# Strided attention: weight columns that interleave two head parities, and stores of every second row in 16 KiB reads

## The chip, the core and the metric

The kernel runs on one core of one Trainium2 chip. The metric is the device time of one execution in microseconds, median of three runs. The core has five engines that run side by side and wait for each other through semaphores: TensorE (PE, matrix products into PSUM; its weight loads are PEld in the profile), VectorE (DVE), ScalarE (ACT), GpSimd (POOL) and SyncE (SP), which here only issues DMA transfers. Sixteen DMA engines move data between DRAM and SBUF, the on-chip memory of 128 partitions.

## The reference

Eight batches of twelve heads, 1024 queries of 64 numbers each. Every query attends to the same 16 keys of its head, at positions 0, 64, ..., 960. All is float32 in DRAM.

```python
batch, heads, seq, dim = (8, 12, 1024, 64)          # stride 64
attend_positions = np.arange(0, seq, stride)        # 16 keys
scores = einsum('bhqd,bhkd->bhqk', q, k) / sqrt(dim)
weights = exp(scores - max); weights /= sum(weights) + 1e-10
result[:, :, i, :] = einsum('bhqk,bhkd->bhqd', weights, v)
```

Q is 25.2 MB and the result is 25.2 MB. Of K and V only 16 rows a head are read, 0.39 MB each.

## The kernel before

The 96 heads are worked on in 24 groups of four heads (HG = 4). A group's Q is 1 MiB: 128 partitions of 8 KiB in tile `qn`. The result of a group is as large: `out_sb`, also 8 KiB in each of 128 partitions.

**Layout.** The four heads of a group are numbered 0 to 3; the parity `a` of a head is its number modulo two. A head has 64 blocks of 16 queries. In `qn` a partition holds 32 queries of one head, so two blocks (x); a block falls into two halves (e) of eight queries (t). In `out_sb`, partition 64a + q holds block q of the two heads of parity a, 4 KiB for each. So in `store` (L250) one partition is read as 8 KiB and written as two pieces of 4 KiB, 512 KiB apart in DRAM, and the 128 partitions form one regular row of steps.

**A group's chain.** `cast` (L199, GpSimd) turns Q into bf16. `transpose` (L203, VectorE) transposes blocks of 32 by 32 pairs of bf16 numbers. `scores` (L205) makes four matmuls of 512 columns (L210) that add up in one PSUM bank: 64 partitions for each parity, and columns ordered by query t, then x, then q, the partition from which the query came. ScalarE takes the exponential of each half (L221) and writes it into the weight buffer `w`: eight matrices of 128 by 128, in which the rows of parity a fill only the columns of parity a, 64a and up; the rest was set to zero once. `values` (L191, GpSimd) lays the values side by side for the four combinations of head and half that a parity has, each in the rows of its own keys, with four more columns of ones that give the sums. `outputs` (L228) multiplies in three blocks, for 3, 2 and 3 of the eight t (L235): column p of a weight matrix becomes partition p of the product. For each block VectorE takes the reciprocal of the sums (L243); in the blocks of three it also multiplies and writes to `out_sb` (L245), and in the block of two ScalarE copies (L247) and GpSimd multiplies (L248). PSUM has two buffers for these products, so the third block's matmuls wait for the first block's L245.

**Order.** The schedule is written by hand. SyncE issues K, load 0, V and loads 1 to 7 at once (QBUFS = 8). Loads 0 and 1 read 128 rows of 8 KiB, later ones 32 rows of 32 KiB (L93). In the loop over g, `ahead(g)` puts in transpose(g + 2), scores(g + 1), values(g + 2) and cast(g + 3), then come the three `outputs`, then `store(g)` and `load(g + 8)`. All transfers leave from one queue, so a load stands behind the store ahead of it. A store waits on SyncE until all three blocks of its group are written. A group's first write to `out_sb` waits for the store of nine groups earlier (OBUFS = 9). In five of the groups from 1 to 7 the keys of later groups are prepared as well (L156 to L169), and in group 4 the second half of the values (L177).

The softmax here doesn't subtract the row's maximum and nothing guards it: scores larger than these inputs give would overflow.

## Time and profile before

| | |
|---|---|
| time, median of three (range) | 129.17 us (128.92 to 129.61) |
| span of the profiled execution | 127.6 us |
| busy: PE, DVE, ACT, POOL | 67.2, 95.5, 57.5, 90.3 us |
| DMA: packets, bytes, mean rate | 7910, 51.19 MB, 401 GB/s |
| issue to landing, median: loads, stores | 11.7, 9.8 us |
| first and last issue of a store | 20.6, 119.9 us |

The profiler's span is shorter than the measured time by some 1.6 us (the profiled execution took 129.27 us). The stretch rows of the page cut the span in 40 slices and give the busy share of each in tenths; PEclk is the clock that TensorE was granted. The rows of groups give, for one line of code, count, busy time, mean duration and the idle time of the engine before it. The timeline gives start and duration of single instructions, and in brackets the engine's idle time before one and what ended it. For a DMA issue the trace also tells how long it took from issue to landing; transfers of one queue land in the order of their issue here. The page's groups that the change touches:

```profile
L235 PE MATMUL o_ps<-v,w 128*128 128x260 bf16 x192 | 40.0, 333 | 36.1 <-DVE out_sb L245 34.5
L221 ACT ACTIVATE w<-sc 64x512 bf16<-64x512 f32 x48 | 35.3, 735 | 30.1 <-PE sc L210 28.3
L210 PE MATMUL sc<-qt,k_t 128*128 128x512 bf16 x96 | 33.3, 479 | 12.8 <-DVE qt L203 11.6
```

### The profile page before, as it was taken

What the parts mean: (1) busy time and instruction counts of PE and PEld (TensorE: products, weight loads), DVE (VectorE), ACT (ScalarE), POOL (GpSimd) and SP (SyncE); (2) the same over time, 40 slices, a digit from 0 to 9 for tenths busy, and PEclk for the clock granted to TensorE, in tenths of its full rate; (3) what the DMA queues carried; (4) which work ended last, traced back from release to release, by engine and by line L of the source; (5) the groups of instructions that cost most, each with busy time, mean ns of one, the idle gap of its engine ahead of it and who ended that gap; (6) DMA issues with size and microseconds to landing.
All of it is one profiled execution on the core that took longest, in us unless ns stands there. A gap on an engine that the chain in (4) does not pass through costs nothing.

```text
span 127.6 us, 1150 instructions
## 1 busy us (share of the span) xinstructions
PE 67.2 (53%) x292; PEld 30.1 (24%) x292; DVE 95.5 (75%) x167; ACT 57.5 (45%) x96; POOL 90.3 (71%) x89
## 2 busy tenths in 40 slices
PE   0005267766456796436757565379734877365100
PEld 0002032233222343212423232124221433132000
DVE  6947557788898678898879888897889878977300
ACT  4110614576771458776445653543554626462100
POOL 8962489877898286898888888898689887433300
PEclk9999999999955558999756999955999657998555
DMA  2999989898998998999989989999999999999980
GB/s 68 378 319 468 462 360 483 349 483 362 460 465 352 480 455 339 506 385 393 501 344 447 460 375 450 426 403 457 442 380 455 439 393 421 424 426 424 429 360 26
DMA packets 7910, 51.19 MB, mean 401 GB/s; under 512 B 3872, under 2 KB 3872, under 8 KB 3872
## 3 DMA queue, kind: packets, MB, share of 16 engines
q1 hardware_dynamic: 7904, 51.12, 96.7%
q8 instruction: 2, 0.03, 0.1%
q14 instruction: 4, 0.03, 0.1%
HBM read 25.95 MB, written 25.17 MB: 401 GB/s over the span
## 4 chain that ended last, share of the span: by engine, by line
DVE 48%; DMA 16%; PE 14%; issue 9%; POOL 4%; SPq 1%; ACT 0%; DVEq 0%; POOLq 0%
DVE out_sb L245 30%; PE o_ps L235 11%; DVE qt L203 10%; DMA out_dram<-out_sb 9%; DMA qn<-in_Q_dram 7%; DVE rec L243 7%; PE sc L210 3%; POOL out_sb L248 2%; POOL qb L199 1%; DVE v_rep L184 1%; SPq L35 1%; POOL v L191 1%; ACT out_sb L247 0%; SPq L100 0%; DVE k_r L159 0%
## 5 line engine op out<-in xcount | busy, mean ns | idle before, releaser
L235 PE MATMUL o_ps<-v,w 128*128 128x260 bf16 x192 | 40.0, 333 | 36.1 <-DVE out_sb L245 34.5
L221 ACT ACTIVATE w<-sc 64x512 bf16<-64x512 f32 x48 | 35.3, 735 | 30.1 <-PE sc L210 28.3
L199 POOL CAST qb<-qn 128x2048 bf16<-128x2048 f32 x24 | 45.3, 1889 | 4.2 <-DMA qn<-in_Q_dram 4.2
L245 DVE TENSOR_TENSOR out_sb<-o_ps,rec 128x768 f32<-128x768 f32 x48 | 46.0, 958 | 1.7
L248 POOL TENSOR_TENSOR out_sb<-out_sb,rec 128x512 f32<-128x512 f32 x24 | 25.0, 1042 | 22.2 <-ACT out_sb L247 22.2
L210 PE MATMUL sc<-qt,k_t 128*128 128x512 bf16 x96 | 33.3, 479 | 12.8 <-DVE qt L203 11.6
L235 PEld LDWEIGHTS <-w 128*128 128x128 bf16 x192 | 18.7, 113 | 63.5 <-DVE out_sb L245 48.1
L203 DVE STREAM_TRANSPOSE qt<-qb 128x1024 int32<-128x1024 int32 x24 | 29.6, 1233 | 4.7 <-POOL qb L199 4.7
L243 DVE RECIPROCAL rec<-o_ps 128x12 f32<-128x12 f32 (+1 forms) x72 | 15.3, 212 | 15.9 <-PE o_ps L235 15.8
L247 ACT COPY out_sb<-o_ps 128x512 f32<-128x512 f32 x24 | 14.0, 585 | 24.9 <-DVE rec L243 12.1
L191 POOL TENSOR_TENSOR v<-mask,v_rep 128x256 bf16<-128x256 bf16 x24 | 16.0, 669 | 2.3 <-DVE v_rep L184 2.3
L210 PEld LDWEIGHTS <-k_t 128*128 128x128 bf16 x96 | 10.8, 113 | 23.8 <-issue 10.7
L169 ACT COPY k_t<-k_r 32x128 bf16<-32x128 bf16 x20 | 5.9, 295 | 2.2 <-DVE k_r L159 1.9
L129 POOL MEMSET k_t<- 128x4608 bf16 x1 | 3.9, 3937 | 0.0
L180 PE MATMUL vp<-v_bf,perm_v 128*128 128x384 bf16 x4 | 1.8, 513 | 2.4 <-DVE v_rep L184 2.4
L139 DVE TENSOR_SCALAR s_sel<-col,slot_f 128x4 bf16<-128x4 int16 x1 | 2.5, 2546 | 0.1
L158 ACT CAST k_bf<-k_raw 128x256 bf16<-128x256 f32 x3 | 1.2, 405 | 3.1 <-DMA k_raw<-in_K_dram 3.0
L184 DVE CAST v_rep<-vp 128x384 bf16<-128x384 f32 x4 | 2.1, 543 | 0.6 <-PE vp L180 0.6
L123 DVE MEMSET k_t<- 128x1152 uint32 x1 | 1.0, 1018 | 1.0 <-PEq L311 1.0
L158 ACT ACT_TABLE_LOAD x1 | 1.3, 1283 | 0.7 <-PEq L311 0.7
L127 DVE MEMSET w<- 128x512 uint32 x3 | 1.5, 485 | 0.2
L118 POOL COPY perm_v<-identity 128x32 bf16<-128x32 bf16 x8 | 1.2, 209 | 0.0
(16 smaller groups left out, 5.0 us busy)
## 6 DMA issues: line engine op xcount, KB each, us to landing
qn<-in_Q_dram SPq DMA_DIRECT2D x24, 1024.0 KB, 11.7
out_dram<-out_sb SPq DMA_DIRECT2D x24, 1024.0 KB, 9.8
k_raw<-in_K_dram SPq DMA_DIRECT2D x1, 384.0 KB, 4.3
v_raw<-in_V_dram SPq DMA_DIRECT2D x1, 384.0 KB, 7.3
```

The costliest lines, as they stand in the source:

```text
L129: nc.gpsimd.memset(k_t[:, 8:NG], 0.0)
L169: op(k_t[dst : dst + 32, 8 * m + c : 8 * m + 8 : 2, :, col : col + NK], k_r[src : src + 32, 4 * m : 4 * m + 4].rearrange("p n (a k f) -> p ...
L191: nc.gpsimd.tensor_tensor(out=vb[g][:, 0 : 4 * D].rearrange("p (s d) -> p s d", s=4), in0=mask, in1=v_rep[:, g // 2, g % 2].unsqueeze(1).t ...
L199: nc.gpsimd.tensor_copy(out=qb[g], in_=qn[g])
L203: nc.vector.transpose(qt[g].bitcast(I32), qb[g].bitcast(I32))
L210: nc.tensor.matmul(sc, lhsT=k_t[:, g, f, NK * (1 - e) : NK * (1 - e) + P], rhs=_ap_with(q, [q.ap[0], [D, 8], [16 * D, 2], [2, 32]], extra_ ...
L221: nc.scalar.activation(out=_ap_with(wa, [wa.ap[0], [P, 8], [1, 2], [2, 32]], extra_offset=64 * a), in_=sc[64 * a : 64 * a + 64].rearrange( ...
L235: nc.tensor.matmul(ps[:, i, 0 : 4 * D + 4], lhsT=wt[g][:, i0 + i], rhs=vb[g], start=True, stop=True,)
L243: nc.vector.reciprocal(r, ps[:, 0:n, 4 * D : 4 * D + 4])
L245: nc.vector.tensor_tensor(out=to, in0=o, in1=by, op=ALU.mult)
L247: nc.scalar.copy(to, o)
L248: nc.gpsimd.tensor_tensor(out=to, in0=to, in1=by, op=ALU.mult)
```

## The change

The weight matrices get their columns interleaved: the rows of parity a fill the columns 2q + a. For that the score matmul reads its moving operand in another order (x innermost, in steps of 16 * D elements, that is 2 KiB), so that the score columns come out by t, then by block of 16 queries, and the exponential writes every second column. Partition 2q + a of a group's result now holds block q of parity a.

The result tiles hold two groups: 16 KiB in a partition, four such tiles (OBUFS = 4) in place of nine of 8 KiB. A store takes the partitions of one parity, 64 of them in steps of two, and both groups: 16 KiB read at a time, written as four pieces of 4 KiB. It is 1 MiB as before, and there are still 24. Both stores of a pair are issued after the odd group, each followed by a load. Q gets ten buffers, so that ten loads are issued ahead. The change is for fewer and longer DMA reads.

```diff
-    QBUFS = 8
-    OBUFS = 9
+    QBUFS = 10
+    OBUFS = 4
...
                     rhs=_ap_with(
-                        q, [q.ap[0], [D, 8], [16 * D, 2], [2, 32]],
+                        q, [q.ap[0], [D, 8], [2, 32], [16 * D, 2]],
                         extra_offset=8 * D * e + f,
                     ),
...
             nc.scalar.activation(
-                out=_ap_with(wa, [wa.ap[0], [P, 8], [1, 2], [2, 32]], extra_offset=64 * a),
-                in_=sc[64 * a : 64 * a + 64].rearrange("p (t x q) -> p t x q", t=8, x=2),
+                out=_ap_with(wa, [wa.ap[0], [P, 8], [2, 64]], extra_offset=a),
+                in_=sc[64 * a : 64 * a + 64].rearrange("p (i q) -> p i q", i=8),
                 func=AF.Exp, bias=0.0, scale=scale,
             )
...
         if c == 0:
-            out_sb[g] = out_pool.tile([P, 4, 8, D], FP32, name="out_sb", tag="out_sb")
+            if g % 2 == 0:
+                out_2[g // 2] = out_pool.tile(
+                    [P, 2, 4, 8, D], FP32, name="out_sb", tag="out_sb"
+                )
+            out_sb[g] = out_2[g // 2][:, g % 2]
...
-    def store(g):
-        o = out_sb[g]
+    def store(n, a):
+        o = out_2[n][a : P : 2]
         _copy(
             nc,
-            _ap_with(out, [[16 * D, P], [2 * SD, 2], [1, 16 * D]], g * HG * SD),
-            _ap_with(o, [o.ap[0], [1, 1], [1, 32 * D]]),
+            _ap_with(
+                out, [[16 * D, 64], [2 * SD, 4], [1, 16 * D]],
+                2 * n * HG * SD + a * SD,
+            ),
+            _ap_with(o, [o.ap[0], [1, 1], [1, 64 * D]]),
         )
...
-        store(g)
-        if g + QBUFS < NG:
-            load(g + QBUFS)
+        if g % 2 == 1:
+            for a in range(2):
+                store(g // 2, a)
+                if g - 1 + a + QBUFS < NG:
+                    load(g - 1 + a + QBUFS)
```

## The prediction

> **What bounds the kernel now.** I read the page's DMA rows first:

> ```profile
> DMA  2999989898998998999989989999999999999980
> ...
> DMA packets 7910, 51.19 MB, mean 401 GB/s; under 512 B 3872, under 2 KB 3872, under 8 KB 3872
> ...
> q1 hardware_dynamic: 7904, 51.12, 96.7%
> ```

> The 16 DMA engines are busy from the second slice to the last but one, and the queue's packets fill 96.7% of their time. 7904 less 3872 small ones leaves 4032 large packets. They fit the reads: 24 stores of 128 reads of 8 KiB (3072), loads 0 and 1 of 128 (256) and 22 loads of 32 reads of 32 KiB (704). So a packet is counted per read, and stores are three quarters of the large ones.

> Second, the engines, since a last store can't leave before its data. VectorE over one group, and its last instruction:

> ```profile
> 77.05 0.96 DVE L245 TENSOR_TENSOR out_sb<-o_ps,rec 128x768 f32<-128x768 f32 x1
> 77.92 0.20 DVE L243 RECIPROCAL rec<-o_ps 128x8 f32<-128x8 f32 x1
> 78.61 0.23 DVE L243 RECIPROCAL rec<-o_ps 128x12 f32<-128x12 f32 x1 [0.49 <-PE o_ps L235]
> 78.88 0.96 DVE L245 TENSOR_TENSOR out_sb<-o_ps,rec 128x768 f32<-128x768 f32 x1
> 79.75 1.23 DVE L203 STREAM_TRANSPOSE qt<-qb 128x1024 int32<-128x1024 int32 x1
> 80.91 0.20 DVE L243 RECIPROCAL rec<-o_ps 128x12 f32<-128x12 f32 x1
> 81.14 0.96 DVE L245 TENSOR_TENSOR out_sb<-o_ps,rec 128x768 f32<-128x768 f32 x1
> ...
> 118.82 0.96 DVE L245 TENSOR_TENSOR out_sb<-o_ps,rec 128x768 f32<-128x768 f32 x1
> ```

> A group takes 81.14 - 77.05 = 4.09 us, with one real gap, 0.49 us for the third block's matmuls. No wait for a DMA stands in VectorE's rows after 23 us, so this chain runs by itself to 119.78 us. The chain of waits shows an 11.52 us step "DMA out_dram<-out_sb" at 100.79 us; VectorE is busy all through it, so I don't take it for a stall.

> Third, the end: SyncE's last issue, and the DMA windows behind it (last two columns: DMA share, GB/s):

> ```profile
> 119.86 0.54 SPq L35 DMA_DIRECT2D out_dram<-out_sb  x1
> ...
> 123.00:123.50 0.50, 0.00 (x0) 0.50 1.09 459
> 123.50:124.00 0.50, 0.00 (x0) 0.50 0.52 213
> 124.00:124.50 0.50, 0.00 (x0) 0.50 0.31 131
> 124.50:125.00 0.50, 0.00 (x0) 0.50 0.28 115
> 125.00:125.50 0.50, 0.00 (x0) 0.50 0.08 33
> ...
> DMA to landing us min/median/max: 6.2/6.2/6.2
> ```

> The last line is that store's: it lands at 119.9 + 6.2 = 126.1 us, 0.85 us after the last bytes (middle of 125.0 to 125.5). The store before it (issue 116.6, landing 7.0 us) lands at 123.6. **Both limits meet here**: the DMA has less than 2 us of older work when the last store arrives.

> [...] From the landing of store 8 (59.04 + 10.1 = 69.1) to that of store 15 (88.4 + 15.3 = 103.7), 14 transfers of 1.049 MB take 2.47 us each; from load 23 (89.03 + 17.1 = 106.1) to the end, 8 stores take 2.50 us each, so a load takes 2.44.[...] The trace shows spells at 0.50, named below.[...]

> **The change, part by part.**
> 1. *16 KiB reads.* Per engine, a store goes from 8 reads to 4. A 32-row load has 2 and takes 2.44 us, a store 2.50: (2.50 - 2.44)/6 = 0.010 us a read. A new store would take 2.46; 24 of them save 1.0 us of DMA time. The lower bound is 0 (loads may be faster because of their direction), the upper 1.6 (reading error 0.1 us in each of the landings).
> 2. *Stores in pairs.* The even group's store waits about one group. In the middle this costs nothing: the queue's latency there is 7 to 17 us, and two more loads ahead stand in it. Ten loads end near the issue of pair 0: the tenth large transfer of before, load 8, landed at 21.2 + 10.3 = 31.5, and pair 0 leaves at 27.4. **At the end it costs.** Now 2.1 MB wait for the last multiply instead of 1.05. If compute ends as before, issue is at 119.9. First bytes come about 1.3 us later (the K load is issued at 0.73, its first bytes are counted between 1.75 and 2.00; bounds 1.0 and 1.8). The older work, place 46 of 48, landed at 113.5 + 7.7 = 121.2 before and lands at 120.3 with part 1, so its last bytes are out by 119.4: the DMA idles near 1.8 us. The end is 119.9 + 1.3 + 2 x 2.46 + 0.85 = 127.0 against 126.1: **+0.9 us**.
> 3. *Ten Q buffers, four pairs.* Load 23 moves from place 40 to 38, landing 4.9 us earlier. That removes the cast's last wait for it (0.79 us at 105.5), worth nothing: VectorE's transpose followed its multiply without a gap there. The pair at groups 22 and 23 needs the stores of 14 and 15, place 40, landed at about 105.5; group 22 begins at 113.4. So fewer output buffers cost nothing; behind that wait would stand VectorE and then all stores.
> 4. *Score columns.* L210's moving operand read 32 columns 4 bytes apart[...]. Now neighbouring columns lie 2 KB apart. PE rows of two groups, warm and throttled:

> ```profile
> 78.06 0.51 PE L235 MATMUL o_ps<-v,w 128*128 128x260 bf16 x3 [1.86 <-DVE out_sb L245]
> 78.41 1.06 PE L210 MATMUL sc<-qt,k_t 128*128 128x512 bf16 x4
> ...
> 86.24 0.83 PE L235 MATMUL o_ps<-v,w 128*128 128x260 bf16 x3 [1.05 <-DVE out_sb L245]
> 86.86 1.91 PE L210 MATMUL sc<-qt,k_t 128*128 128x512 bf16 x4
> ```

> Lower bound: no cost, 1.06 us. Middle, which I take: half rate[...]; about 1.9 us warm, and no more than that throttled. Upper: a quarter of the rate, 3.6 us. At 1.9 us all of it lies in the 1.86 us idle before L235: warm, the first block's product would be ready near 80.8 us where VectorE takes it at 80.91. At 3.6 us it would be ready at 82.5, so each of 23 groups gets some 1.6 us longer.
> 5. *Clock.* Spreading the same columns over 1.9 us leaves PE gaps near 1.0 us in place of 1.86[...]. Throttled groups cost: between store issues 4.4 us instead of 4.09 (35.7 to 40.1, 63.2 to 67.5, 84.0 to 88.4, 100.8 to 105.2), then 4.2 in the next one; together 1.6 us. Add about 0.6 in the group of value_rows at 40 us and 0.32 in the last L235 (0.83 for 0.51): 2.5 us at most.
> 6. *Exponential.* Its two writes per group keep a 4-byte step and their count: the same 735 ns, with ACT idle before L221 for 28.3 us in all. Nothing.

> **The cases.**
> - **A, tail exposed, compute as before:** 129.17 + 0.9 = 130.1. For it: nothing in the diff shortens VectorE's chain at full clock. Chance 0.36; variations of the clock spread it over 128.7 to 131.5.
> - **B, clock stays up (forecast):** compute ends up to 2.5 us earlier, the last pair goes out at 117.4, its bytes could come at 118.7, before the older work is out (119.4). Then the DMA never idles and the 1.0 us of part 1 counts: 128.2. For it: more than half the time between 35 and 70 us is throttled, so there is something to win. Against: it needs two steps that no row shows. Chance 0.44.
> - **C, reading at quarter rate:** 23 x 1.6 = 37 less the tail slack, about 165 us. Chance 0.10.
> - **D[...]:**[...] If a store takes 2.7 us, 24 x 0.2 = 4.8, 134 us.[...] With a colder clock (+2 us) counted here: chance 0.10.

> **Numbers.** Predicted: B, 128.2 us. The range runs from 127.4 (B with the upper saving) to 132.5 (A with a late first byte and some throttling); it leaves out C and half of D. Faster by over 0.5% (below 128.52): most of B and a little of A, 0.42. Within 0.5%: 0.15. Slower (above 129.82): most of A, C and D, 0.43.

> **What the next profile would show.** Part 1: packets fall by 24 x 64 = 1536, and landings in the last third come 2.46 us apart. Part 2: the last store issues come 0.6 us apart, and windows before the last 2 MB show a DMA share well under 1 if A holds, near 1 if B does. Part 4: L210 four at a time in 1.9 us at full clock. Part 5: hardly a 5 in the PEclk row, and a last L245 near 117 us. I am wrong if L210 takes 1.06 us and the clock dips as before (A), if VectorE waits longer than 0.49 us for the first block of each group (C), or if landings are over 2.6 us apart (D).

## The result and the profile after

The changed kernel takes **143.34 us** (142.54 to 144.42) against 129.39 us for the kernel before in the same comparison: ratio 1.109, 95% interval 1.100 to 1.117. The forecast was 128.2 us with a range up to 132.5; the kernel became slower by 14 us. One run of e2 (142.80 us) and one of e5 (130.52 us) were slow ones, over 1.5% above the fastest of their kernel, and are left out below.

The clock row of the kernel before, and then, from the page of the changed kernel, its clock and DMA rows, its queue, the chain of steps that ended last, and the cost of the score matmuls:

```profile
PEclk9999999999955558999756999955999657998555
...
PEclk9999999997555555595595559568556997775555
DMA  3999999989989999999999999999996908529185
...
q1 hardware_dynamic: 6368, 51.12, 88.7%
...
PE sc L210 34%; PE o_ps L239 22%; DVE out_sb L249 19%; DMA qn<-in_Q_dram 6%; DVE rec L247 5%; DVE qt L203 2%; POOL qb L199 1%; DVE v_rep L184 1%; SPq L35 1%; POOL v L191 0%; SPq L100 0%; SPq L98 0%; DVEq L247 0%
...
L210 PE MATMUL sc<-qt,k_t 128*128 128x512 bf16 x96 | 56.3, 708 | 12.3 <-DVE qt L203 11.2
```

The packets fell by exactly the 1536 reads that were to go (7904 to 6368 on the queue). But the DMA row now has holes in the last quarter, so there the DMA is no longer what the kernel waits for. L210 went from 479 to 708 ns in the mean, and it leads the chain, with the output matmuls (L239, L235 before) second. The PEclk row shows half speed (5) from slice 11 on in most places: the mean granted clock fell from 0.825 to 0.714.

VectorE over one group, at a throttled spot, and its last instruction:

```profile
75.36 0.96 DVE L249 TENSOR_TENSOR out_sb<-o_ps,rec 128x768 f32<-128x768 f32 x1
76.24 0.20 DVE L247 RECIPROCAL rec<-o_ps 128x8 f32<-128x8 f32 x1
77.25 0.23 DVE L247 RECIPROCAL rec<-o_ps 128x12 f32<-128x12 f32 x1 [0.81 <-PE o_ps L239]
...
80.05 0.23 DVE L247 RECIPROCAL rec<-o_ps 128x12 f32<-128x12 f32 x1 [0.43 <-PE o_ps L239]
80.32 0.96 DVE L249 TENSOR_TENSOR out_sb<-o_ps,rec 128x768 f32<-128x768 f32 x1
...
132.69 0.96 DVE L249 TENSOR_TENSOR out_sb<-o_ps,rec 128x768 f32<-128x768 f32 x1
```

The group takes 80.32 - 75.36 = 4.96 us instead of 4.09. Two waits grew: the one for the third block is 0.81 instead of 0.49 us, because L239's three matmuls run at half clock (0.83 us at a granted clock of 0.50, where they take 0.51 at 1.00); and there is a new wait of 0.43 us for the first block. VectorE's last multiply ends at 133.65 us, 13.9 us later than before. The waits of VectorE for the output matmuls, in us, times and longest, first before and then after:

```profile
DVE rec L243 <- PE o_ps L235: 15.8, 27, 1.0
...
DVE rec L247 <- PE o_ps L239: 27.6, 45, 1.7
```

That is 11.8 of the 13.9 us. The rest fits the overlap that an instruction loses when it has to wait: neighbours on VectorE overlap by some 0.09 us (in the lines above, 75.36 + 0.96 ends after 76.24), there are 18 more waits, and its busy time rose by 1.9 us though the long operations kept their durations.

TensorE in the changed kernel; the reader should set the 2.32 and 2.37 beside the 1.06 and 1.91 of before:

```profile
71.74 0.51 PE L239 MATMUL o_ps<-v,w 128*128 128x260 bf16 x3 [0.89 <-DVE out_sb L249]
72.09 2.32 PE L210 MATMUL sc<-qt,k_t 128*128 128x512 bf16 x4
74.25 1.24 PE L239 MATMUL o_ps<-v,w 128*128 128x260 bf16 x5
76.38 0.83 PE L239 MATMUL o_ps<-v,w 128*128 128x260 bf16 x3 [0.89 <-DVE out_sb L249]
77.00 2.37 PE L210 MATMUL sc<-qt,k_t 128*128 128x512 bf16 x4
```

The single matmul's row has a median of 0.703 us, so four that start 0.54 us apart make 3 x 0.54 + 0.70 = 2.32. Before, 0.388 and 0.224 make 1.06. This start distance is what I call the price of a matmul below. It hardly changes with the clock: 2.32 beside a first row of 0.51 (full clock), 2.37 beside 0.83.

The end, DMA windows of 1 us and the landing of the last two stores (issued at 133.7 and 134.3):

```profile
132.00:133.00 1.00, 0.38 (x2) 0.50 0.00 0
133.00:134.00 1.00, 0.00 (x0) 0.50 0.00 0
134.00:135.00 1.00, 0.00 (x0) 0.50 0.50 213
...
DMA to landing us min/median/max: 4.2/5.2/6.1
```

The DMA has nothing to do for more than two microseconds before the last pair. The exposed tail of case A is there, on top of a compute chain that is 13.9 us longer: the second store's data has landed at 134.3 + 6.1 = 140.4, which is 6.7 us after the pair's first issue.

### The profile page after: what moved, and what is told of

Same layout as the page of the kernel before. It is cut to its first block, busy times and chain, and to the rows that moved or that the text cites. A ratio compares the mean times of both kernels' runs of the same rounds, so it can differ in the third digit from the quotient of the medians.

```text
span 141.4 us, 1125 instructions
## 1 busy us (share of the span) xinstructions
PE 95.0 (67%) x292; PEld 32.9 (23%) x292; DVE 97.4 (69%) x167; ACT 57.7 (41%) x96; POOL 90.3 (64%) x89
## 2 busy tenths in 40 slices
DMA packets 6373, 51.18 MB, mean 362 GB/s; under 512 B 3872, under 2 KB 3872, under 8 KB 3872
## 3 DMA queue, kind: packets, MB, share of 16 engines
q1 hardware_dynamic: 6368, 51.12, 88.7%
## 4 chain that ended last, share of the span: by engine, by line
PE 56%; DVE 26%; DMA 6%; issue 2%; POOL 2%; SPq 1%; DVEq 0%
PE sc L210 34%; PE o_ps L239 22%; DVE out_sb L249 19%; DMA qn<-in_Q_dram 6%; DVE rec L247 5%; DVE qt L203 2%; POOL qb L199 1%; DVE v_rep L184 1%; SPq L35 1%; POOL v L191 0%; SPq L100 0%; SPq L98 0%; DVEq L247 0%
## 5 line engine op out<-in xcount | busy, mean ns | idle before, releaser
L210 PE MATMUL sc<-qt,k_t 128*128 128x512 bf16 x96 | 56.3, 708 | 12.3 <-DVE qt L203 11.2
L239 PE MATMUL o_ps<-v,w 128*128 128x260 bf16 x192 | 44.9, 380 | 23.1 <-DVE out_sb L249 22.8
L221 ACT ACTIVATE w<-sc 64x512 bf16<-64x512 f32 x48 | 35.5, 739 | 53.1 <-PE sc L210 52.5
L239 PEld LDWEIGHTS <-w 128*128 128x128 bf16 x192 | 21.1, 122 | 61.5 <-DVE out_sb L249 33.7
L247 DVE RECIPROCAL rec<-o_ps 128x12 f32<-128x12 f32 (+1 forms) x72 | 15.9, 221 | 27.8 <-PE o_ps L239 27.6
L203 DVE STREAM_TRANSPOSE qt<-qb 128x1024 int32<-128x1024 int32 x24 | 29.6, 1233 | 4.7 <-POOL qb L199 4.7
L251 ACT COPY out_sb<-o_ps 128x512 f32<-128x512 f32 x24 | 14.1, 586 | 15.5 <-DVE rec L247 11.5
L210 PEld LDWEIGHTS <-k_t 128*128 128x128 bf16 x96 | 11.2, 117 | 36.5 <-issue 26.6
```

The lines of the kernel that those rows point to most:

```text
L203: nc.vector.transpose(qt[g].bitcast(I32), qb[g].bitcast(I32))
L210: nc.tensor.matmul(sc, lhsT=k_t[:, g, f, NK * (1 - e) : NK * (1 - e) + P], rhs=_ap_with(q, [q.ap[0], [D, 8], [2, 32], [16 * D, 2]], extra_ ...
L221: nc.scalar.activation(out=_ap_with(wa, [wa.ap[0], [P, 8], [2, 64]], extra_offset=a), in_=sc[64 * a : 64 * a + 64].rearrange("p (i q) -> p ...
L239: nc.tensor.matmul(ps[:, i, 0 : 4 * D + 4], lhsT=wt[g][:, i0 + i], rhs=vb[g], start=True, stop=True,)
L247: nc.vector.reciprocal(r, ps[:, 0:n, 4 * D : 4 * D + 4])
L251: nc.scalar.copy(to, o)
```

## Experiments

**Theory R**: the reading of score columns in turns from places 2 KiB apart costs the time. **Rival S**: the stores of every second row, or the four pairs, do.

### e1_read_undone: the read alone put back

```diff
-   q, [q.ap[0], [D, 8], [2, 32], [16 * D, 2]],
+   q, [q.ap[0], [D, 8], [16 * D, 2], [2, 32]],
...
-   out=_ap_with(wa, [wa.ap[0], [P, 8], [2, 64]], extra_offset=a),
-   in_=sc[64 * a : 64 * a + 64].rearrange("p (i q) -> p i q", i=8),
+   out=_ap_with(wa, [wa.ap[0], [P, 8], [2, 2], [4, 32]], extra_offset=a),
+   in_=sc[64 * a : 64 * a + 64].rearrange("p (t x q) -> p t x q", t=8, x=2),
```

> The changed kernel with the score matmul reading its columns in the old order; the exponential makes the interleaving instead, writing every fourth column in two passes. Stores, pairs and buffers as in the change. Theory R[...]: L210 goes back from 0.70 to 0.39 us a row, the group's period from 4.7 to about 4.1 us, and only the exposed tail of the paired store is left: 130.1 us, between 129 and 131. Rival S (stores of every second row collide, or the four pairs make VectorE wait): stays near 143 us whatever the read costs. If 16 KiB reads are worth anything, landings of the stores come 2.46 us apart where the queue is full, against 2.50 before.

131.24 us (130.6 to 131.75), ratio to before 1.013 (1.006 to 1.020); granted clock 0.809. 12.1 of the 14 us are gone with the stores and buffers of the change still in: S falls as the main cause. The time lies 0.2 us above the band. Two things were not foreseen. The exponential pays for the interleaving in its turn:

```profile
L221 ACT ACTIVATE w<-sc 64x512 bf16<-64x512 f32 x48 | 62.9, 1309 | 23.3 <-PE sc L210 22.3
```

Writing every fourth column takes 1309 ns against 735; in the last groups ScalarE's copy (L251) stands behind it. The last multiply ends at 121.2 instead of 119.8 us; about half of this delay arises in those groups, the rest was there before them. And the tail, in windows of 0.5 us:

```profile
120.00:120.50 0.50, 0.00 (x0) 0.50 0.24 98
...
121.50:122.00 0.50, 0.00 (x0) 0.50 0.00 0
122.00:122.50 0.50, 0.00 (x0) 0.50 0.54 229
```

The DMA is idle from about 120.1 to 122. The eight stores behind load 23, up to place 46, can be read for the rate: load 23 lands at 101.5, place 46 at 121.3, so 19.8 / 8 = 2.48 us each against 2.50. Each landing is read to 0.1 us, so this stands for 2.46 to 2.49.

### e2_read_alone: the kernel before with the new read only

```diff
-   q, [q.ap[0], [D, 8], [16 * D, 2], [2, 32]],
+   q, [q.ap[0], [D, 8], [2, 32], [16 * D, 2]],
...
-   out=_ap_with(wa, [wa.ap[0], [P, 8], [1, 2], [2, 32]], extra_offset=64 * a),
-   in_=sc[64 * a : 64 * a + 64].rearrange("p (t x q) -> p t x q", t=8, x=2),
+   out=_ap_with(wa, [wa.ap[0], [P, 8], [1, 64]], extra_offset=64 * a),
+   in_=sc[64 * a : 64 * a + 64].rearrange("p (i q) -> p i q", i=8),
```

> The kernel before with the new order of the score columns alone; the weights stay in blocks by parity, stores and buffers as before. Theory R: the period is 4.7 us as in the changed kernel, and the tail is one store of 1 MiB and not two, so about 2.4 us less than the changed kernel: 141 us. Rival S: 129 to 130 us. The granted clock tells whether the slow read throttles TensorE by itself: about 0.71 if so, about 0.82 if the clock falls for another cause.

140.69 us (139.98 to 140.87), ratio 1.085 (1.077 to 1.093), L210 again 708 ns, clock 0.728. The read by itself costs 11.4 us and brings the low clock with it. Its last store is alone and meets an empty queue: issued at 133.3, it lands 4.2 us later. (The exponential, which writes neighbouring columns here, takes 592 ns.)

### e3_tail_split: e1 with the last pair stored by group

```diff
-        if g % 2 == 1:
+        if g >= NG - 2:
+            for a in range(2):
+                store_one(g, a)      # 64 partitions, 8 KiB reads, 512 KiB
+        elif g % 2 == 1:
             for a in range(2):
```

> As e1_read_undone, but the last pair is stored by group and parity, four transfers of 512 KiB in 8 KiB reads, so that the last but one group's result leaves when it is done. If the tail of e1 is the wait of the last pair, this ends 0.9 to 1.5 us before e1: 128.2 to 129.2 us. If the DMA queue is full to the end in e1 anyway, it equals e1.

129.50 us (129.05 to 130.23), ratio 1.0016 (0.9996 to 1.0036), just above the band: 1.74 us less than e1. Its last multiply ends no earlier than e1's (121.6 against 121.2), so the gain lies in the tail. It is not all the price of the pair: the last transfers here are half as large as a store of before, so the last one is also shorter. Without the late pair and without the slow read the change is even with the kernel before.

### e8_change_with_columns: the change with more TensorE work

```diff
+        if c == 1:
+            pad = psum_sc.tile([P, 512], FP32, name="pad", tag="sc")
+            for i in range(2):
+                nc.tensor.matmul(
+                    pad, lhsT=wt[g][:, 0], rhs=qt[min(g + 1, NG - 1)][:, 0:512], start=True, stop=True
+                )
```

> The changed kernel with two more matmuls of 512 contiguous columns for each group, put behind the second block's matmuls, where TensorE waits 0.9 to 1.1 us for VectorE; their product is not used. They take 0.43 us at full clock, so at full clock nothing waits for them. Theory: part of the loss is the clock, which the slow read drags down[...]. Then the granted clock rises from 0.71 to about 0.9, groups of 4.95 us become 4.5 us, and the time falls by some 4 to 5 us to about 139 us; what is left is the read alone. If the clock follows TensorE's busy time instead (67% of the span in the changed kernel, 53% before), it is not held down by idleness, the clock stays near 0.71 and the time at 143 us or above.

134.63 us (134.3 to 134.77), ratio 1.036 (1.034 to 1.039), clock 0.942. **More work made the changed kernel 8.7 us faster**, twice what was expected. Its clock row and one group:

```profile
PEclk9999999999998698699959999999999999999975
...
72.58 0.51 PE L239 MATMUL o_ps<-v,w 128*128 128x260 bf16 x3 [0.67 <-DVE out_sb L255]
72.93 2.33 PE L210 MATMUL sc<-qt,k_t 128*128 128x512 bf16 x4
75.09 0.72 PE L239 MATMUL o_ps<-v,w 128*128 128x260 bf16 x5
...
76.90 0.51 PE L239 MATMUL o_ps<-v,w 128*128 128x260 bf16 x3 [0.67 <-DVE out_sb L255]
```

The period is 76.90 - 72.58 = 4.32 us. The slow read is unchanged at 2.33; but the five L239 matmuls behind it take 0.72 instead of the 1.24 us that stand at 74.25 in the changed kernel, so VectorE finds the first block almost ready: the wait of 0.43 us was made by the clock as well, not by the read alone. The 4.5 us that were expected of a group at full clock were too long. Against the 4.09 us of before, 0.23 us a group are left, the read's own price.

### e4_more_columns: the same on the kernel before

```diff
-        for e in range(2):
-            for f in range(2):
+        for e, f in ((0, 0), (1, 1), (0, 0), (0, 1), (1, 0), (1, 1)):
```

> The kernel before with two of the four score matmuls of each group issued twice (the first two are overwritten by the restart of the sum). 0.43 us more of TensorE work for each group at full clock, at the full rate of columns; the first block would be ready at 80.3 where VectorE takes it at 80.9, so at full clock nothing waits. If real columns keep the clock up: granted clock over 0.9, compute ends 2 us earlier, and the time is held by the DMA, 128.5 to 129.2. If not, the clock stays at about 0.82 and throttled groups get longer: 130 to 132 us.

129.26 us (128.92 to 129.85), ratio 0.999 (0.997 to 1.001), clock 0.936:

```profile
PEclk9999999999997799999999999999999999959555
```

Hardly a dip is left, and the time is unchanged: the landings show places 46, 47 and 48 at 121.5, 124.0 and 126.4 us, within 0.4 us of before. One thing came otherwise than expected: the last multiply ends at 121.3 us and not 2 us before 119.8. Compute ran ahead until it had no free output tile, and GpSimd's multiply waited for a store:

```profile
117.10 1.04 POOL L248 TENSOR_TENSOR out_sb<-out_sb,rec 128x512 f32<-128x512 f32 x1 [4.11 <-DMA out_dram<-out_sb]
```

So the DMA holds the kernel before. On the clock, the runs together say this. A group has 4 x 512 + 8 x 260 = 4128 columns, and 1024 more in e4 and e8.

| kernel | columns / us of a group at full clock | columns per us | granted clock |
|---|---|---|---|
| change, e2 | 4128 / 4.32 | 956 | 0.714, 0.728 |
| before | 4128 / 4.09 | 1009 | 0.825 |
| e8 | 5152 / 4.32 | 1193 | 0.942 |
| e4 | 5152 / 4.09 | 1260 | 0.936 |

(The 4.32 us are e8's period; e2 has it too where its clock is full, from 85.9 to 90.3 us.) A low clock makes a group still longer and so its columns still fewer in a us (4.96 us, 832, at a clock of 0.50 in the changed kernel). TensorE's busy time does not order the kernels: it was busy 67% of the span in the changed kernel, 53% before and in e4. Nor does the gap before the first output matmul: 0.89 us in the changed kernel, 1.86 before. That columns in a stretch of time keep the clock up is inferred from this order; how the throttle counts is not shown.

### Four reads of the same number of columns

What does the price hang on? The kernel before with other orders of the columns, where only the order of the rows of the result, or in pair16 the queries as well, is another. A place is where in a partition of Q the next column is read; the change and the last two orders read from two places in turns. In pair16 each of the two gives four columns before both go on by 32 bytes.

```diff
-   q, [q.ap[0], [D, 8], [16 * D, 2], [2, 32]],
+   q, [q.ap[0], [16 * D, 2], [2, 2], [4, 128]],     # p8: steps of 8 bytes
+   q, [q.ap[0], [16 * D, 2], [2, 4], [8, 64]],      # p16: steps of 16 bytes
+   q, [q.ap[0], [16, 64], [2, 4], [8, 2]],          # pair16: two places 16 bytes apart
+   q, [q.ap[0], [2, 4], [8, 64], [16 * D, 2]],      # alt2k: 2 KiB apart, on by 16 bytes
```

> The kernel before with the score matmul's columns read in steps of 8 bytes[...]. The rows of the result come in another order; nothing else is changed.[...] between full rate (0.22 us a matmul at full clock, as before) and 0.27 us; the time stays within 1 us of before. If it is the step[...], it grows with the step: some 0.3 us.

> As p8_two_per_line with steps of 16 bytes[...].[...] as slow as the pairs 2 KiB apart of the change, 0.54 us a matmul, L210 0.70 us in the mean, and about 141 us. If the distance of 2 KiB between neighbours matters[...], it is well under 0.54 us, nearer the 0.22 of before.

> [...] The columns come in another order and partly from other queries. Steps of 4, 8 and 16 bytes took 0.22, 0.45 and 0.91 us a matmul, the change 0.54. Reuse theory[...]: about 0.54 us and 140 us of time. Distance theory[...]: 0.9 us and about 175 us.

> The kernel before with score columns that alternate between two places 2 KiB apart and go on by 16 bytes after each pair[...]. The rows of the result come in another order. Reuse theory: 0.9 us a matmul, about 175 us. Distance theory: 0.54 us, about 140 us.

Four score matmuls in each, from the timelines of p8, p16, pair16 and alt2k in this order:

```profile
80.19 1.97 PE L210 MATMUL sc<-qt,k_t 128*128 128x512 bf16 x4
...
88.36 3.79 PE L210 MATMUL sc<-qt,k_t 128*128 128x512 bf16 x4
...
81.56 2.37 PE L210 MATMUL sc<-qt,k_t 128*128 128x512 bf16 x4
...
84.91 4.04 PE L210 MATMUL sc<-qt,k_t 128*128 128x512 bf16 x4
```

| order of columns | places in turns | a place goes on by | price, us | time, us |
|---|---|---|---|---|
| before | 1 | 4 bytes | 0.22 | 129.4 |
| p8 | 1 | 8 bytes | 0.45 | 129.2 |
| p16 | 1 | 16 bytes | 0.90 | 177.3 |
| change | 2, 2 KiB apart | 4 bytes | 0.54 | 143.3 |
| pair16 | 2, 16 bytes apart | 4 bytes | 0.54 | 142.5 |
| alt2k | 2, 2 KiB apart | 16 bytes | 0.97 | 183.5 |

Prices are (length of the four less median of one) / 3, as above. p8, p16, pair16 and alt2k were run once each. The first two expectations missed: p8 was to be at most 0.27, p16 no worse than the change. The second pair of runs then decided between step ("reuse") and distance: two near places cost the same 0.54 as two far ones when each goes on by 4 bytes, and two far places that go on by 16 bytes cost 0.97, one place 0.90. **Between 16 bytes and 2 KiB the distance of two places made no difference (0.54 in both); what counted is the step by which a place goes on (0.54 with 4 bytes, 0.97 with 16).** Two places in turns instead of one added 0.32 us with steps of 4 bytes, 0.07 with 16. With one place the price doubles with the step from 4 to 8 and from 8 to 16 bytes: 0.44, 0.88 and 1.76 ns a column (0.224, 0.45 and 0.90 / 512). In turns between two places that go on by 4 bytes, a column costs about 1.05 ns in the mean (0.54 / 512). Where in TensorE's read this price arises is not shown. p8 doubles the price and yet stays at 129.2 us: 1.97 us fits into TensorE's idle time. The change's 2.32 does not, at the clock that it gets. p8 also has the columns per us of before with TensorE busier (62% of the span), and its clock, 0.857, lies in the spread of before (0.82 to 0.87 in all runs but one). A step over 16 bytes was not run.

For p16 and alt2k a clock of 1.0 is listed, but their traces hold no record of the clock at all, and their pages have no PEclk row. L235's three matmuls take 0.83 us there in every group, the duration that goes with half clock elsewhere. So they probably ran at half clock, which is not shown. The price can be compared all the same if it follows the clock as little as in p8 (four in 1.97 us at full clock, 1.99 at half) and in the change; their times hold a loss from the clock too.

### Could the idea be saved?

e5_plain_pairs keeps the old columns and stores a pair as one transfer of 2 MiB on all 128 partitions, with the first and last two groups by themselves. e6_plain_pairs_clock adds e4's matmuls to e5; e7_interleaved_best adds them to e3 and splits the first pair too.

```diff
-    QBUFS = 8
-    OBUFS = 9
+    QBUFS = 10
+    OBUFS = 4
...
+    def store_pair(n):
+        o = out_2[n]
+        _copy(
+            nc,
+            _ap_with(out, [[16 * D, P], [2 * SD, 4], [1, 16 * D]], 2 * n * HG * SD),
+            _ap_with(o, [o.ap[0], [1, 1], [1, 64 * D]]),
+        )
```

> The kernel before (columns, layout and read order as there) with result tiles of two groups, ten Q buffers and four pairs, in which the pairs 1 to 10 leave as one store of 2 MiB on all 128 partitions in 16 KiB reads, and the first and last two groups by themselves. Nothing interleaves. If the 16 KiB reads are worth 0.03 us a transfer as in e1_read_undone, 1.0 us of DMA time is saved; compute ends at 119.5 or so as before, and the last store is alone after it, so most of the gain is lost to compute: 128.2 to 129.3 us.

129.34 us (128.46 to 129.95), ratio 0.999 (0.997 to 1.001).

> As e5_plain_pairs with two of the four score matmuls issued twice, which raised the granted clock from 0.82 to 0.94 in e4_more_columns. Both limits are then eased: compute ends 2 us earlier and the DMA needs 1 us less: 127.5 to 128.5 us. If the DMA saving is not real, it equals e4: 129.2 us.

129.09 us (128.55 to 129.57), ratio 0.998 (0.997 to 1.000). The last multiply ends at 116.7 us, 3.1 us earlier than before, and the time hardly moves: again the DMA holds it. Place 46 lands at 121.7 us in e5 and in e6, no earlier than the 121.2 of before: the gain of 1.0 us is not there. Stores in a row come 4.9 us a pair, 2.45 us a MiB, which is better than 2.50; but in the middle, where loads and stores mix, four MiB take 9.8 to 10.1 us, no better than before (4 x 2.47 = 9.9).

> As e3_tail_split, with the first pair also stored by group and parity (the DMA queue ran thin there between 34 and 40 us in e1_read_undone: gaps of 2.8 and 3.2 us between landings) and with two of the four score matmuls issued twice for the clock. If the interleaved 16 KiB stores save 0.03 us a transfer as in e1_read_undone and nothing else is short: 127.8 to 128.6 us. If the DMA is the limit at the same total as before: 129.1 us, like e6_plain_pairs_clock.

130.69 us (129.96 to 131.67), ratio 1.010 (1.006 to 1.014), a miss. Clock 0.921, but two landings in the first half come 3.5 and 4.2 us after the one ahead (loads behind pairs that were late), and the last multiply ends at 122.2 us behind the long exponentials. No version here beats the kernel before by more than e6's 0.2%.

## Why the prediction was wrong

- **Part 4, the price of the read, was mis-sized: 1.9 us forecast, 2.32 measured.** Half rate was an estimate of mine that no run of before showed. The runs give 0.45 us for steps of 8 bytes against 0.22, 0.90 for steps of 16, and the change with its two places is neither: 0.54. The step "all of it lies in the 1.86 us idle before L235" failed by that 0.4 us, and because it reckoned the five output matmuls at full clock. At 1.97 us it holds (p8, 129.2 us). At 2.32 and full clock a group takes 0.23 us longer (e8), some 5 us in 23 groups; with the clock that came of it, 0.87 (4.96 against 4.09).
- **Part 5, the clock, went the other way**, and this is the larger error. I argued that a longer, more even L210 leaves shorter gaps and so a higher clock. That was an estimate of mine, shown by no trace of before; the measurement is that the clock was 0.50 from 74.3 to 84.4 us of the changed kernel with no gap over 0.89 us. A slow matmul fills the gap in the trace but brings no more columns: 0.714. e8 prices it: of 14 us, 8.7 go with the clock. Case B stood on this step.
- **The mechanism of case C was the right one** (VectorE waits for the first block), with a chance of 0.10 and at a quarter of the rate, about 165 us. I had listed three prices and nothing between 1.9 and 3.6; a price of 2.3 with a falling clock was in no case, and so not in the range.
- **Part 2, the tail, had the right mechanism.** It was forecast at 0.9 us with compute as before. e1 lands its last store 1.8 us later than before (127.9 for 126.1), of which 1.4 us is its later last multiply (121.2 for 119.8), so the pair costs 0.4 there. First bytes came about 1 us after issue (in the changed kernel issue at 133.7 us, DMA share 0.00 up to 134.9, the first bytes counted before 135.0), within the bounds. From first issue to landing the pair takes 6.6 us in e1 and 6.7 in the changed kernel; what differs is the single store in its place: 6.2 us behind older work (before), 4.2 with an empty queue (e2). Where compute comes last, the pair costs 6.7 - 4.2 = 2.5 us.
- **Part 1 was right in the count (1536) and wrong in the worth.** 2.46 a store was close to e1's 2.48 (2.46 to 2.49), yet no kernel ended earlier for it. In e1 the queue ran thin between 34 and 40 us, in e5 the mixed stretch is no faster. Why, is not settled.
- **Parts 3 and 6 held.** VectorE has no wait for an output buffer in the changed kernel, and L221 takes 739 ns.
- **Case D fell:** 64 partitions in steps of two move at 2.48 us a MiB (e1), not 2.7.

The time adds up: 11.4 us for the read with its clock (e2) and 2.5 for the last pair make 13.9, and 13.95 were measured.

## What to carry to other kernels

The reordering was paid in both places here: in TensorE's read it cost 0.32 us a matmul (0.54 for 0.22), in ScalarE's write 574 ns an instruction (1309 for 735); first look whether another transfer shape (one plain store of the pair) makes it unnecessary. A slower read that seems to fit into TensorE's idle time must be reckoned with the clock that follows from it: in these runs columns in a stretch of time told the clock (0.714 at 956 columns per us, 0.942 at 1193), and busy time did not (67% at 0.714, 53% at 0.825 and 0.936). Before shortening transfers, find what the last transfer waits for, since merging two stores puts both behind the last multiply (2.5 us here).
